# Decoder layer with mixture of experts: the loop for further rounds in front of the last expert group, and joint stores

## The chip, the cores and the metric

The kernel runs on one core of a Trainium2 chip. The metric is device time in microseconds of one execution; the runs before took 459.01 to 460.41 us, median 459.82. Engines are TensorE (PE; its weight loads are PEld), VectorE (DVE), ScalarE (ACT), GpSimd (POOL) and SyncE (SP), which issues most DMAs from one in-order queue.

## The reference

One decoder layer for 256 tokens of width 1024, in float32:

```
h  = RMSNorm(x);  [u|v|q|k|vb] = h @ W_in
y_a = u * (tril(W_s) RMSNorm(v) + b)          # chunks of 128
y_b = differential attention of q, k, vb       # 8 heads, ALiBi, softmax1 - lam*softmax2
x  = x + (sigmoid(h Wg_a)*(y_a Wup_a) + sigmoid(h Wg_b)*(y_b Wup_b)) @ W_out
t  = RMSNorm(x);  group = top-1 of 4, experts = top-2 of the 8 in it
y  = sum over experts e of c[e] * (silu(t w1[e]) * (t w3[e])) @ w2[e]     # 32 experts, hidden 256
out = x + y
```

## The kernel before

**The front.** Projections, mixers, gates and the output projection run as units of weight pieces, each split into a high and a low part. They end near 258 us and are not touched by the change.

**The experts.** The 32 experts are worked in eight groups of four (`run_groups`, `group`). A group takes for each expert at most 32 tokens (`SL`). Its steps, in `group`: `sel` makes a 0/1 matrix `Sg` of tokens by slots on VectorE; `gather` multiplies it with the token rows, which gives the gathered tokens `hT` (two halves of four pieces); `products` multiplies `hT` with w1 and w3, in eight steps `kc` of one weight chunk each, into `h` (L1123); then `hid` (silu on ScalarE, product on VectorE), two transposes `pt`, the copy `hidT`, and the second stage: four chunks of w2 give `y` (L1170), copied to `yy` (L1176), and `comb` scatters it back onto the PSUM banks `res` with the matrix `SwT` (L1149). `back_a` (GpSimd) makes `Sw`, the weighted `Sg`, and `back_b` transposes it to `SwT`. Parts of the next group's preparation are hung into the steps of a group by the table `mids`: entry `kc` runs behind product `kc`, entry `KC + i` behind chunk `i` of the second stage.

**The weight stream.** A group has 12 chunks of 1 MB, 96 in all; I number them 0 to 95, so the last group has 84 to 95. `Stream.pump` issues a transfer on SyncE whenever a slot is free. From chunk 54 on, two chunks go together as one 2 MB transfer into one of six double buffers `sd_70` to `sd_75` (L162), a "double"; chunk 94 is a transfer of its own (L174) and chunk 95 two halves (L156). Chunks 86/87 go to `sd_75`, 88/89 to `sd_70`, 90/91 to `sd_71`, 92/93 to `sd_73`.

**The last group.** It also stores the result: behind each range of 256 or 128 columns, `put_out` copies `res` to a tile `out` (VectorE, in the last ranges also ScalarE) and stores it: six stores in all. Behind each of its product steps 0 to 6 stand 14 matmuls on constants (`warm`, L275), 18 behind step 7; nothing reads their result.

**Further rounds.** An expert with more than 32 tokens needs another round. The kernel counts on the chip how many are needed (`ci`, made in the first group); behind everything each engine loads that count and, if it is over zero, loops over all eight groups again and stores the result once more. With these inputs the loop is not entered. The order of the instructions in front of the loop is written out by hand (`manual_schedule`): each engine works in the order of the code.

Of the kernel before, what the change touches and what calls it, by code (L numbers as in the profile page):

```python
# [7 lines left out]
F32 = mybir.dt.float32  # L8
# [9 lines left out]
P = 128  # L18
D = 1024
T = 256  # L20
NT = 2
KC = 8
# [19 lines left out]
RESERVE = (6, 3, 2, 0, 0, 0, 0, 0, 1)  # L42
SL = 32
NW = (14, 18)

COLS = (((0, 256),), ((512, 256),), ((256, 128), (768, 128)), ((384, 128), (896, 128)))
NGRP = 8
NCH = 12
ROUNDS = T // SL
# [81 lines left out]
def piece(chunk, e):  # L131

    return chunk[e] if isinstance(chunk, tuple) else chunk[:, e * 512:(e + 1) * 512]
# [66 lines left out]
def body(tc, cp, sp, tp, mmp, axp, xT_d, xn_d, wf_d, wm_d, wst_d, bs_d, pv_d, rb_d, wr_d, out_d):  # L200
    nc = tc.nc
    V, S, G, TE = nc.vector, nc.scalar, nc.gpsimd, nc.tensor
    slots = Slots(sp, "s", NSLOT - 3 - 2 * NTWO, NTWO)
# [5 lines left out]
    def ax_ps(name):  # L209
        return axp.tile([P, 512], F32, tag="ax", name=name)  # L210
# [24 lines left out]
    def t1k(shape, name, dt=F32):  # L235
        return tp.tile(shape, dt, tag="t1k", name=name, bufs=6)
# [4 lines left out]
    order = tc.manual_schedule()  # L241
# [3 lines left out]
    stream = Stream(nc, slots, [wf_d[i] for i in range(40)], wm_d, 40 + TWO)  # L245
# [4 lines left out]
    first = [stream.claim() for _ in range(NFIRST)]  # L250
    for a, b in FIRST:
        c = slice(a % 4 * 512, (b - 1) % 4 * 512 + 512)
# [19 lines left out]
    def warm(n):  # L272
        wps = ax_ps("wps")
        for _ in range(n):
            TE.matmul(wps[:, :P], ones_b, ones_b, start=True, stop=True)  # L275
# [8 lines left out]
    for sl_, base in ((slice(0, P), 0), (slice(P, 3 * P), -P)):  # L284
        n = sl_.stop - sl_.start
# [86 lines left out]
    A = {}  # L372
# [495 lines left out]
    res = [[None] * 2 for _ in range(NT)]  # L868
# [171 lines left out]
            evac0(part)  # L1040


    def put_out(c, n):

        o = slots.take([P, NT, n], F32, "out")
        for t in range(NT):
            src = res[t][c // 512][:, c % 512:c % 512 + n]
            if t == 0 and (c, n) in COLS[-1]:
                S.copy(o[:, t], src)
            else:  # L1050
                V.tensor_copy(o[:, t], src)
        nc.sync.dma_start(out_d[0, :, c:c + n].rearrange("(t p) n -> p t n", t=NT), o)
        slots.drop(o)

    def group(g, chunks, done, mid, store):

        es = slice(g * 4, g * 4 + 4)
        st = {"h": [None, None]}

        def sel(ts=range(NT)):  # L1060
            if 0 in ts:
                st["S"] = t1k([P, NT, 4, SL], f"Sg{g}")
            for t in ts:
                V.tensor_tensor(st["S"][:, t], io32p[:, None, :].to_broadcast([P, 4, SL]),  # L1064
                                pos_m[:, t, es, None].to_broadcast([P, 4, SL]), ALU.is_equal)
# [9 lines left out]
                      start=start, stop=t == NT - 1, skip_group_check=True)  # L1075

        def gather_T(hf):
            st["h"][hf] = A["lp"].tile([P, 4, P], F32, tag=f"h{hf}", name=f"hT{g}{hf}")

        def gather_out(hf, ps, ks):  # L1080
            n = len(ks)
# [36 lines left out]
        def products():  # L1118
            ps = ax_ps(f"h{g}")
            for kc in range(KC):  # L1120
                w = chunks()
                for e in range(4):
                    TE.matmul(ps[e * SL:(e + 1) * SL], st["h"][kc // 4][:, kc % 4, e * SL:(e + 1) * SL], piece(w, e),  # L1123
                              start=kc == 0, stop=kc == KC - 1)
                done()
                if store and kc < KC - 1:
                    warm(NW[0])
                for f in mid.get(kc, ()):
                    f()
            if store:  # L1130
                warm(NW[1])
            hid = t1k([P, T], f"hid{g}")
            S.activation(hid, ps[:, :256], AF.Silu)  # L1133
            V.tensor_tensor(hid, hid, ps[:, 256:], ALU.mult)  # L1134
            for f in mid.get("act", ()):
                f()
            pt = ax_ps(f"pt{g}")
            for f in range(2):
                TE.transpose(pt[:, f * P:(f + 1) * P], hid[:, f * P:(f + 1) * P], ident)
            hidT = t1k([P, 2, P], f"hidT{g}")  # L1140
            V.tensor_copy(hidT, pt[:, :256].rearrange("p (f s) -> p f s", f=2))
            for f in mid.get("T", ()):
                f()

            def comb(ranges, yy):
                o = 0
                for c, n in ranges:
                    for t in range(NT):
                        TE.matmul(res[t][c // 512][:, c % 512:c % 512 + n], st["SwT"][:, t * P:(t + 1) * P], yy[:, o:o + n],  # L1149
                                  start=False, stop=True, skip_group_check=True)  # L1150
                    o += n
                    if store:
                        put_out(c, n)

            last = None
            for i, ranges in enumerate(COLS):
                chunk = chunks()
                final = g == NGRP - 1 and i == 3
                o = 0
                for part in [(r,) for r in ranges] if final else [ranges]:  # L1160
                    n = sum(r[1] for r in part)
                    py = ax_ps(f"y{g}{i}{o}")
                    if final:
                        v = chunk[:, o * 8:(o + n) * 8].rearrange("p (e f n) -> p e f n", e=4, f=2)
                        w = [v[:, e] for e in range(4)]
                    else:
                        w = [piece(chunk, e).rearrange("p (f n) -> p f n", f=2) for e in range(4)]
                    for f in range(2):
                        for e in range(4):
                            TE.matmul(py[e * SL:(e + 1) * SL, :n], hidT[:, f, e * SL:(e + 1) * SL], w[e][:, f],  # L1170
                                      start=f == 0, stop=f == 1)
                    o += n
                    if o == 256:
                        done()
                    yy = t1k([P, n], f"yy{g}{i}{o}")
                    S.copy(yy, py[:, :n])  # L1176
                    if last:
                        comb(*last)
                    last = (part, yy)
                    if store and i == 1:  # L1180
                        comb(*last)
                        last = None
                for f in mid.get(KC + i, ()):
                    f()
            if last:
                comb(*last)

        return sel, gather, back_a, back_b, products, gather0, evac0, sel_r2

    def run_groups(next_, done_, first, final):  # L1190
        mids = [{} for _ in range(NGRP)]
        gr = [group(g, next_, done_, mids[g], final and g == NGRP - 1) for g in range(NGRP)]
        sel, gather, back_a, back_b, _, gather0, evac0, sel_r2 = gr[0]
        if first:
            choice_end(sel, gather0, evac0, sel_r2)
        else:
            sel()
            gather(0)
        mids[0][2] = [lambda: gather(1, "Sr" if first else "S")]
        mids[0][3] = [first, back_a] if first else [back_a]  # L1200
        if first:
            mids[0][4] = [lambda t=t: res_init(t, 1) for t in range(NT)]
        mids[0][6] = [back_b]
        for g in range(NGRP):
            if g + 1 < NGRP:
                sel_, gather_, back_a_, back_b_ = gr[g + 1][:4]
                mids[g].setdefault(4, []).append(sel_)

                mids[g]["act"] = [lambda ga=gather_: ga(0)]
                mids[g]["T"] = [lambda ga=gather_: ga(1)]  # L1210
                mids[g][KC + 2] = [back_a_]
                mids[g + 1][1] = [back_b_]
            gr[g][4]()

    def consume(st):

        box = {}

        def next_():
            box["w"] = st.next()  # L1220
            return box["w"]

        def done_():
            slots.drop(box["w"])
            st.pump(0)
        return next_, done_

    ci = cp.tile([P, 1], I32, name="ci")

    def rest():  # L1230
# [11 lines left out]
        V.tensor_reduce(cs, cr, AX.X, ALU.add)  # L1242
        V.tensor_copy(ci, cs)

    run_groups(*consume(stream), rest, True)
    order.__exit__(None, None, None)


    more = nc.values_load(ci[0:1, 0:1], min_val=0, max_val=ROUNDS - 1)
    with tc.If(more > 0):  # L1250
        with tc.For_i(0, more, 1):
            V.tensor_scalar(pos_m, pos_m, -float(SL), None, ALU.add)
            st = Stream(nc, slots, [], wm_d, 0)
            st.pump(0)
            run_groups(*consume(st), None, False)
        for ranges in COLS:
            for c, n in ranges:
                put_out(c, n)
    for name in ("gathered", "extra2", "gates", "extra"):
        close_pool(name)  # L1260

# [62 lines left out]
```

## Time and profile before

| | |
|---|---|
| runs | 459.01 to 460.41 us, median 459.82 |
| profiled execution | 459.95 us, its span 458.2 us |
| busy: TensorE, VectorE, ScalarE, GpSimd | 433.5, 219.6, 184.2, 94.7 us |
| DMA | 148.75 MB, mean 325 GB/s over the span |
| last double landed | 443.53 us |
| end of the last copy | 452.2 us |

Times within the profile count from the start of the span. A view of a stretch lists for each engine the busy time and the number of instructions, then the granted share of TensorE's clock (1.00 is 2.4 GHz, 0.50 is 1.2 GHz). In a list of operations, "[0.41 <-DMA ...]" is the idle time in front and what ended it.

### The profile page before, as it was taken

To read this page: it belongs to the slowest core of one execution; us is meant where nothing else is said; L and a number is where in the kernel's file an instruction comes from. 1 tells how busy PE (TensorE), PEld (TensorE's weight loads), DVE (VectorE), ACT (ScalarE), POOL (GpSimd) and SP (SyncE) were. 2 spreads that over 40 slices of the span, in tenths; PEclk is the share of its full clock that TensorE was granted. 3 is DMA by queue.
4 is the path that set the end of the run, shared out by engine and by line. 5 is a ranking of instruction groups with operands and counts; after the bars stand their busy time and mean duration, and the time that the engine had idled before them with its cause. 6 is when DMAs were issued, how large, how long until landed. Compare 5 with 4: busy or idle time off the path is not lost.

```text
span 458.2 us, 7864 instructions
## 1 busy us (share of the span) xinstructions
PE 433.5 (95%) x3136; PEld 317.8 (69%) x3136; DVE 219.6 (48%) x423; ACT 184.2 (40%) x364; POOL 94.7 (21%) x120
## 2 busy tenths in 40 slices
PE   8999999999999999999999999999999968759984
PEld 6787778878999888888888845475554625307553
DVE  4865696779897766666885633021110201001012
ACT  5946557676565776644565233010100101001001
POOL 1057576446567000004000111000000000000000
PEclk9999999999999999999999999999999999968998
DMA  7999943554327877698776999999999999999993
GB/s 265 415 421 423 406 151 137 183 185 149 129 93 276 349 294 275 240 377 297 297 257 209 393 358 426 418 418 421 406 425 424 428 426 426 426 429 428 423 378 106
DMA packets 23129, 148.75 MB, mean 325 GB/s; under 512 B 2736, under 2 KB 5040, under 8 KB 9136
## 3 DMA queue, kind: packets, MB, share of 16 engines
q1 hardware_dynamic: 22656, 147.91, 81.1%
q8 instruction: 26, 0.43, 0.4%
q10 hardware_dynamic: 432, 0.28, 0.2%
q14 instruction: 15, 0.12, 0.1%
HBM read 147.14 MB, written 1.05 MB: 323 GB/s over the span
## 4 chain that ended last, share of the span: by engine, by line
PE 74%; DMA 20%; DVE 2%; POOL 1%; ACT 1%; issue 1%; SPq 0%
DMA sd<-in_wm_dram 16%; PE h L1123 9%; PE gp L1074 5%; PE y L1170 4%; PE res L1149 4%; PE b L467 3%; PE gb L467 3%; PE ga L467 3%; PE a L467 3%; DMA sd<-in_xn_dram 2%; PE v L419 2%; PE u L448 2%; PE u L449 2%; PE u L450 2%; PE ga L468 2%; PE b L468 2%
## 5 line engine op out<-in xcount | busy, mean ns | idle before, releaser
L404 DVE TENSOR_TENSOR hl<-sd,hl 128x1024 fp32r<-128x1024 f32 (+2 forms) x84 | 87.4, 1046 | 43.0 <-ACT hl L400 40.8
L400 ACT CAST hl<-sd 128x1024 fp32r<-128x1024 f32 (+1 forms) x84 | 80.4, 965 | 63.2 <-PE a L468 8.5
L1123 PE MATMUL h<-sd,hT 128*32 128x512 f32 x384 | 49.9, 630 | 13.8 <-DMA sd<-in_wm_dram 13.8
L1134 DVE TENSOR_TENSOR hid<-hid,h 128x256 f32<-128x256 f32 x8 | 3.4, 422 | 99.2 <-ACT hid L1133 99.2
L406 POOL TENSOR_TENSOR hl<-sd,hl 128x352 fp32r<-128x352 f32 x32 | 40.4, 1274 | 20.8 <-ACT hl L400 20.6
L1176 ACT COPY yy<-y 128x256 f32<-128x256 f32 (+1 forms) x33 | 12.1, 366 | 68.4 <-PE y L1170 68.3
L1123 PEld LDWEIGHTS h<-sd,hT 128*32 128x32 f32 x384 | 10.7, 112 | 38.5 <-issue 19.1
L1109 POOL TENSOR_TENSOR Sw<-Sg,C 128x128 f32<-128x128 f32 x16 | 6.1, 399 | 149.6 <-PE res L1149 140.0
L1149 PE MATMUL res<-yy,SwT 128*128 128x128 f32 (+1 forms) x192 | 34.6, 323 | 0.1
L1074 PEld LDWEIGHTS gp<-Sg,acc 128*128 128x128 f32 x240 | 29.1, 198 | 7.5 <-issue 7.5
L1149 PEld LDWEIGHTS res<-yy,SwT 128*128 128x128 f32 x192 | 25.9, 190 | 10.5 <-issue 6.0
L1074 PE MATMUL gp<-Sg,acc 128*128 128x128 f32 x240 | 31.2, 285 | 0.0
L1133 ACT ACTIVATE hid<-h 128x256 f32<-128x256 f32 x8 | 3.1, 383 | 56.4 <-PE h L1123 56.4
L467 PE MATMUL ga<-x,hl 128*128 128x512 f32 x64 | 22.8, 400 | 0.0
L467 PE MATMUL b<-yb,hl 128*128 128x512 f32 x64 | 22.7, 399 | 0.0
L467 PE MATMUL gb<-x,hl 128*128 128x512 f32 x64 | 22.7, 399 | 0.0
L467 PE MATMUL a<-ya,hl 128*128 128x512 f32 x64 | 22.7, 399 | 0.0
L1170 PE MATMUL y<-sd,hidT 128*32 128x256 f32 x304 | 19.3, 383 | 1.7 <-DMA sd<-in_wm_dram 1.7
L1082 DVE TENSOR_TENSOR hT<-gp,pv 128x512 f32<-128x512 f32 (+1 forms) x19 | 11.3, 606 | 19.9 <-PE gp L1074 19.9
L1064 DVE TENSOR_TENSOR Sg<-io32p,pos_m 128x128 f32<-128x128 f32 x16 | 4.0, 288 | 33.1 <-PE y L1170 33.1
L448 PE MATMUL u<-x,hl 128*128 128x256 f32 x64 | 18.8, 293 | 0.0
L450 PE MATMUL u<-x,hl 128*128 128x256 f32 x64 | 18.1, 283 | 0.0
(226 smaller groups left out, 901.0 us busy)
## 6 DMA issues: line engine op xcount, KB each, us to landing
sd<-in_wm_dram SPq DMA_DIRECT2D x20, 2048.0 KB, 24.1
sd<-in_wf_dram SPq DMA_DIRECT2D x34, 1024.0 KB, 6.4
sd<-in_wm_dram SPq DMA_DIRECT2D x27, 1024.0 KB, 7.9
w<-in_wm_dram SPq DMA_DIRECT2D x24, 1024.0 KB, 10.2
w<-in_wm_dram SPq DMA_DIRECT2D x16, 256.0 KB, 8.9
sd<-in_wf_dram SPq DMA_DIRECT2D x6, 512.0 KB, 7.6
sd<-in_xn_dram SPq DMA_DIRECT2D x2, 1024.0 KB, 9.1
w<-in_wf_dram SPq DMA_DIRECT2D x2, 1024.0 KB, 8.1
```

Of the source, the lines that this page charges most:

```text
L400: S.copy(hl[:, 0, c], raw[:, c])
L404: V.tensor_tensor(hl[:, 1, c.start:m], raw[:, c.start:m], hl[:, 0, c.start:m].bitcast(F32), ALU.subtract)
L406: G.tensor_tensor(hl[:, 1, m:c.stop], raw[:, m:c.stop], hl[:, 0, m:c.stop].bitcast(F32), ALU.subtract)
L448: TE.matmul(o, wh, a[:, 0], start=kc == 0, stop=False)
L450: TE.matmul(o, wl, a[:, 0], start=False, stop=kc == KC - 1)
L467: TE.matmul(ps, wh, a.rearrange("p c t -> p (c t)"), start=kc == 0, stop=False, skip_group_check=True)
L468: TE.matmul(ps[:, :T], wl, a[:, 0], start=False, stop=kc == KC - 1, skip_group_check=True)
L1074: TE.matmul(ps[:, i * P:(i + 1) * P], h2[:, t, kc * P:(kc + 1) * P], st[S_][:, t].rearrange("p e s -> p (e s)"), start=start, stop=t == NT ...
L1123: TE.matmul(ps[e * SL:(e + 1) * SL], st["h"][kc // 4][:, kc % 4, e * SL:(e + 1) * SL], piece(w, e), start=kc == 0, stop=kc == KC - 1)
L1149: TE.matmul(res[t][c // 512][:, c % 512:c % 512 + n], st["SwT"][:, t * P:(t + 1) * P], yy[:, o:o + n], start=False, stop=True, skip_group_ ...
L1170: TE.matmul(py[e * SL:(e + 1) * SL, :n], hidT[:, f, e * SL:(e + 1) * SL], w[e][:, f], start=f == 0, stop=f == 1)
L1176: S.copy(yy, py[:, :n])
```

## The change

Four edits. The last group is cut off from `run_groups` and emitted behind the loop (`last_group`); the count is loaded in group 4 (`count`), and the branch stands between groups 6 and 7. What the last group holds over the loop (its `Sg` and `hT`, and the tiles for the output) gets slots of its own, and the loop's weights use those that are left. Four of the six output ranges are copied into one tile and stored in two transfers, one for each half of the tokens. The matmuls on constants behind steps 0 to 5 of the last group go, and its `back_a` and `back_b` move to its steps 1 and 4.

```diff
+NW_FROM = 6
...
     def put_out(c, n):
-        o = slots.take([P, NT, n], F32, "out")
+        h, k = divmod(c, 512)
+        late = (c, n) in COLS[-1]
         for t in range(NT):
-            src = res[t][c // 512][:, c % 512:c % 512 + n]
-            if t == 0 and (c, n) in COLS[-1]:
-                S.copy(o[:, t], src)
+            src = res[t][h][:, k:k + n]
+            if late and t == 0:
+                S.copy(out_t[c][:, t], src)
+            elif late:
+                V.tensor_copy(out_t[c][:, t], src)
             else:
-                V.tensor_copy(o[:, t], src)
-        nc.sync.dma_start(out_d[0, :, c:c + n].rearrange("(t p) n -> p t n", t=NT), o)
-        slots.drop(o)
+                V.tensor_copy(out_t[0][:, t, h, k:k + n], src)
+        if late:
+            nc.sync.dma_start(out_d[0, :, c:c + n].rearrange("(t p) n -> p t n", t=NT), out_t[c])
+        elif (c, n) == COLS[-2][-1]:
+            o = out_d[0].rearrange("(t p) (h n) -> p t h n", t=NT, h=2)
+            for t in range(NT):
+                nc.sync.dma_start(o[:, t, :, :k + n], out_t[0][:, t])
...
-                st["S"] = t1k([P, NT, 4, SL], f"Sg{g}")
+                st["S"] = slots.take([P, NT, 4, SL], F32, f"Sg{g}") if store else t1k([P, NT, 4, SL], f"Sg{g}")
...
-                if store and kc < KC - 1:
+                if store and NW_FROM <= kc < KC - 1:
                     warm(NW[0])
...
+        if count:
+            mids[4][6] = [count]
...
-                mids[g][KC + 2] = [back_a_]
-                mids[g + 1][1] = [back_b_]
+                if first and g + 2 == NGRP:
+                    mids[g + 1][1] = [back_a_]
+                    mids[g + 1][4] = [back_b_]
+                else:
+                    mids[g][KC + 2] = [back_a_]
+                    mids[g + 1][1] = [back_b_]
+            elif first:
+                return gr[g][4]
             gr[g][4]()
...
-    run_groups(*consume(stream), rest, True)
+    def count():
+        more.append(nc.values_load(ci[0:1, 0:1], min_val=0, max_val=ROUNDS - 1))
+
+    last_group = run_groups(*consume(stream), rest, count)
+    take_out()
     order.__exit__(None, None, None)
-    more = nc.values_load(ci[0:1, 0:1], min_val=0, max_val=ROUNDS - 1)
-    with tc.If(more > 0):
-        with tc.For_i(0, more, 1):
+    with tc.If(more[0] > 0):
+        with tc.For_i(0, more[0], 1):
             V.tensor_scalar(pos_m, pos_m, -float(SL), None, ALU.add)
-            st = Stream(nc, slots, [], wm_d, 0)
+            st = Stream(nc, slots, [], wm_d, NGRP * NCH)
             st.pump(0)
-            run_groups(*consume(st), None, False)
-        for ranges in COLS:
-            for c, n in ranges:
-                put_out(c, n)
+            run_groups(*consume(st), None)
+    order = tc.manual_schedule()
+    order.__enter__()
+    last_group()
+    order.__exit__(None, None, None)
```

SyncE's queue from the double with chunks 86/87 (`sd_75`) on, before; what stands in brackets are the semaphores that an instruction waits for (`DMAHW` those of transfers, the others those of engines):

```order
L162 DMA sd_75<-in_wm_dram 128x4096 [waits DMAHW0_49,PE_49]
L162 DMA sd_70<-in_wm_dram 128x4096 [waits DMAHW1_49,PE_49]
L162 DMA sd_71<-in_wm_dram 128x4096 [waits DMAHW2_49,PE_49]
L162 DMA sd_73<-in_wm_dram 128x4096 [waits DMAHW3_49,PE_49]
L174 DMA w_3742<-in_wm_dram 128x2048
L156 DMA w_3744<-in_wm_dram 128x1024
L156 DMA w_3744<-in_wm_dram 128x1024 [waits DMAHW4_49]
L1052 DMA out_dram<-out_3980 128x2x256 [waits DMAHW5_49,DVE_49]
...
L1249 TENSOR_LOAD ci [waits DVE_49]
L1249 ISA x2
...
L1052 DMA out_dram<-out_4043 128x2x128 [waits DMAHW2_49,DVE_49,Activation_49]
L1250 COMPARE_AND_BRANCH
```

The same place now; the loop's path (the rows left out) is skipped when the count is zero, and the branch with the eight `DMAHW` waits is the path that skips it:

```order
L163 DMA sd_75<-in_wm_dram 128x4096 [waits DMAHW0_49,PE_49]
L1284 COMPARE_AND_BRANCH
...
L1284 UNCONDITIONAL_BRANCH [waits DMAHW0_49,DMAHW1_49,DMAHW2_49,DMAHW3_49,DMAHW4_49,DMAHW5_49,DMAHW6_49,DMAHW7_49]
L163 DMA sd_70<-in_wm_dram 128x4096 [waits DMAHW7_49,DMAHW1_49,PE_49]
L163 DMA sd_71<-in_wm_dram 128x4096 [waits DMAHW2_49,DMAHW0_49,PE_49]
L163 DMA sd_73<-in_wm_dram 128x4096 [waits DMAHW3_49,DMAHW1_49,PE_49]
L175 DMA w_3756<-in_wm_dram 128x2048 [waits DMAHW2_49]
L157 DMA w_3758<-in_wm_dram 128x1024 [waits DMAHW3_49]
L157 DMA w_3758<-in_wm_dram 128x1024 [waits DMAHW4_49]
L1063 DMA out_dram<-out_3797 256x1x384 [waits DMAHW5_49,DVE_49]
...
L1059 DMA out_dram<-out_3798 128x2x128 [waits DMAHW7_49,DVE_49,Activation_49]
```

The transfers of chunks 88 to 95 and the stores stood in front of the branch; they now stand behind it, and behind a wait for every transfer issued so far.

TensorE at the start of the last group, before: products `h` of the first chunk, then the matmuls on constants `wps`:

```order
L1149 MATMUL res_2818<-yy_3776,SwT_3659 128x128
L1149 MATMUL res_2821<-yy_3776,SwT_3659 128x128
L1123 MATMUL h_3786<-sd_74,hT_3703 32x512 [waits DMAHW5_49,PE_49]
L1123 MATMUL h_3786<-sd_74,hT_3703 32x512 x3
L275 LDWEIGHTS ones_b
L275 MATMUL wps<-ones_b 128x128 [waits PE_49]
L275 LDWEIGHTS ones_b
```

TensorE now, from the end of the path that skips the loop to the first matmuls on constants:

```order
L1284 UNCONDITIONAL_BRANCH [waits PE_49]
L1141 MATMUL h_5201<-sd_74,hT_111_3717 32x512 [waits DVE_49,DMAHW5_49,PE_49,Activation_49]
L1141 MATMUL h_5201<-sd_74,hT_111_3717 32x512 x7
L1141 MATMUL h_5201<-sd_75,hT_111_3717 32x512 [waits DMAHW6_49]
L1141 MATMUL h_5201<-sd_75,hT_111_3717 32x512 x7
L1141 MATMUL h_5201<-sd_70,hT_112_3733 32x512 [waits DMAHW7_49]
L1141 MATMUL h_5201<-sd_70,hT_112_3733 32x512 x3
L1132 MATMUL pw_5225<-ident,Sw_5210 128x128 [waits Pool_49] x2
L1141 MATMUL h_5201<-sd_70,hT_112_3733 32x512 x4
L1141 MATMUL h_5201<-sd_71,hT_112_3733 32x512 [waits DMAHW0_49]
L1141 MATMUL h_5201<-sd_71,hT_112_3733 32x512 x3
L276 LDWEIGHTS ones_b [waits PE_49]
L276 MATMUL wps<-ones_b 128x128 [waits Activation_49]
```

The first product now follows the branch, six sets of `wps` are gone, and `pw` (`back_b`) moved from behind the second chunk to behind the fifth.

## Rows read from the trace of the kernel before

**Rows 1.** the page, part 2: tenths of busy time or clock in forty equal slices

```profile
PEclk9999999999999999999999999999999999968998
DMA  7999943554327877698776999999999999999993
```

**Rows 2.** the chain that ended last, 405 to 460: start us, us, what

```profile
408.89 3.64 PE h L1123 x16
...
419.57 23.96 DMA sd<-in_wm_dram
...
443.67 1.93 PE y L1170 x32
...
451.95 0.28 DVE out L1051
```

**Rows 3.** SyncE's timeline, each followed by its issues: KB each, us to landing

```profile
401.08 0.33 SPq L162 DMA_DIRECT2D sd<-in_wm_dram  x1
...
sd<-in_wm_dram SPq DMA_DIRECT2D x1, 2048.0 KB, 27.6
...
420.43 0.91 SPq L156 DMA_DIRECT2D w<-in_wm_dram  x2
...
w<-in_wm_dram SPq DMA_DIRECT2D x2, 512.0 KB, 27.2
```

**Rows 4.** TensorE's timeline, 394 to 452: start us, us, operation, idle before

```profile
399.09 1.92 PE L1123 MATMUL h<-sd,hT 128*32 128x512 f32 x16 [2.35 <-DMA sd<-in_wm_dram]
...
425.55 1.06 PE L1123 MATMUL h<-sd,hT 128*32 128x512 f32 x8
426.55 0.95 PE L275 MATMUL wps<-ones_b 128*128 128x128 bf16 x14
...
433.78 1.06 PE L1123 MATMUL h<-sd,hT 128*32 128x512 f32 x8 [0.41 <-DMA sd<-in_wm_dram]
...
438.67 1.06 PE L1123 MATMUL h<-sd,hT 128*32 128x512 f32 x8 [1.05 <-DMA sd<-in_wm_dram]
...
441.56 1.18 PE L275 MATMUL wps<-ones_b 128*128 128x128 bf16 x18
```

**Rows 5.** stretches: us, busy (x instructions) by engine, PEclk, DMA share, GB/s

```profile
360.00:380.00 20.00, 15.84 (x157) 6.94 (x155) 1.19 (x3) 1.86 (x5) 0.76 (x2) 1.00 1.01 427
...
393.50:404.60 11.10, 4.82 (x42) 1.40 (x46) 0.00 (x0) 0.37 (x1) 0.00 (x0) 1.00 1.01 428
404.60:414.90 10.30, 8.48 (x43) 3.25 (x32) 0.42 (x1) 0.38 (x1) 0.00 (x0) 0.50 1.01 426
414.90:425.50 10.60, 10.60 (x113) 7.55 (x111) 1.71 (x3) 1.49 (x4) 0.76 (x2) 1.00 1.01 427
425.50:435.30 9.80, 9.39 (x110) 4.61 (x109) 0.00 (x0) 0.37 (x1) 0.00 (x0) 1.00 1.00 425
```

**Rows 6.** the branch's lines L1249 and L1250: ns min/median/max, first and last start

```profile
L1249 SPq TENSOR_LOAD <-ci x1: 481/481/481, 451.0 to 451.0; - x1
...
L1250 SPq EVENT_SEMAPHORE  x8: 17/17/17, 453.4 to 456.8; - x8
...
L1250 PEldq COMPARE_BRANCH  x1: 4253/4253/4253, 452.1 to 452.1; - x1
...
L1250 SPq COMPARE_BRANCH  x1: 50/50/50, 452.9 to 452.9; - x1
```

**Rows 7.** DMA, 451 to 457, then the stores issued at 450.1 and 452.4

```profile
DMA  8986985000005995887210010000000000000005
...
q8 instruction: 2, 0.03, 3.3%
q14 instruction: 3, 0.02, 1.2%
...
out_dram<-out SPq DMA_DIRECT2D x1, 128.0 KB, 1.9
...
out_dram<-out SPq DMA_DIRECT2D x1, 128.0 KB, 4.0
```

More of the change, by code (lines that the diff above doesn't have):

```diff
@@ L1040, in choice_end, with take_out @@
             evac0(part)
+    out_t = {}
     def put_out(c, n):
-        o = slots.take([P, NT, n], F32, "out")
+        h, k = divmod(c, 512)
+        late = (c, n) in COLS[-1]
         for t in range(NT):
-            src = res[t][c // 512][:, c % 512:c % 512 + n]
-            if t == 0 and (c, n) in COLS[-1]:
-                S.copy(o[:, t], src)
-            else:
-                V.tensor_copy(o[:, t], src)
-        nc.sync.dma_start(out_d[0, :, c:c + n].rearrange("(t p) n -> p t n", t=NT), o)
-        slots.drop(o)
+            src = res[t][h][:, k:k + n]
[3 more added lines that the diff above has]
+                V.tensor_copy(out_t[c][:, t], src)
+            else:
+                V.tensor_copy(out_t[0][:, t, h, k:k + n], src)
[5 more added lines that the diff above has]
+                nc.sync.dma_start(o[:, t, :, :k + n], out_t[0][:, t])
+    def take_out():
+        c, n = COLS[-2][-1]
+        out_t[0] = slots.take([P, NT, 2, c % 512 + n], F32, "out")
+        for c, n in COLS[-1]:
+            out_t[c] = slots.take([P, NT, n], F32, "out")
     def group(g, chunks, done, mid, store):
@@ L1077, in gather_T @@
         def gather_T(hf):
-            st["h"][hf] = A["lp"].tile([P, 4, P], F32, tag=f"h{hf}", name=f"hT{g}{hf}")
+            st["h"][hf] = (slots.take([P, 4, P], F32, f"hT{g}{hf}") if store else
+                           A["lp"].tile([P, 4, P], F32, tag=f"h{hf}", name=f"hT{g}{hf}"))
         def gather_out(hf, ps, ks):
@@ L1188, in group, with run_groups @@
         return sel, gather, back_a, back_b, products, gather0, evac0, sel_r2
-    def run_groups(next_, done_, first, final):
+    def run_groups(next_, done_, first, count=None):
         mids = [{} for _ in range(NGRP)]
-        gr = [group(g, next_, done_, mids[g], final and g == NGRP - 1) for g in range(NGRP)]
+        gr = [group(g, next_, done_, mids[g], first and g == NGRP - 1) for g in range(NGRP)]
         sel, gather, back_a, back_b, _, gather0, evac0, sel_r2 = gr[0]
@@ L1243, in rest @@
         V.tensor_copy(ci, cs)
-    run_groups(*consume(stream), rest, True)
+    more = []
+    def count():
+        more.append(nc.values_load(ci[0:1, 0:1], min_val=0, max_val=ROUNDS - 1))
+    last_group = run_groups(*consume(stream), rest, count)
+    take_out()
     order.__exit__(None, None, None)
-    more = nc.values_load(ci[0:1, 0:1], min_val=0, max_val=ROUNDS - 1)
-    with tc.If(more > 0):
-        with tc.For_i(0, more, 1):
+    with tc.If(more[0] > 0):
+        with tc.For_i(0, more[0], 1):
             V.tensor_scalar(pos_m, pos_m, -float(SL), None, ALU.add)
-            st = Stream(nc, slots, [], wm_d, 0)
+            st = Stream(nc, slots, [], wm_d, NGRP * NCH)
             st.pump(0)
-            run_groups(*consume(st), None, False)
-        for ranges in COLS:
-            for c, n in ranges:
-                put_out(c, n)
+            run_groups(*consume(st), None)
[3 more added lines that the diff above has]
+    order.__exit__(None, None, None)
     for name in ("gathered", "extra2", "gates", "extra"):
```

## The prediction

> **What bounds the kernel now.** I read the page's forty slices first: from slice 23 on the DMA row stands at nine tenths until the last slice, and PEclk is full except for a dip in slices 36 and 37 and the very end [rows 1]. Then the chain that ended last: its two long pieces near the end are weight transfers, the last one until 443.53, and what follows is the tail of products, stores and barrier [rows 2]. So the last 200 us run at the rate of the weight stream, and the end is that stream's last double chunk (92 and 93) plus what TensorE, ScalarE, VectorE and the stores still do behind it: 443.67 to 458.2, 14.5 us.
>
> Third, the issues. The double with chunks 86 and 87 is issued at 401.08 and lands 27.6 us later, at 428.7; the last piece of chunk 95 is issued at about 420.9 and lands some 27.2 us later, at 448.1 to 448.5 [rows 3]. The queue thus holds five transfers ahead of use and never runs empty: 8 MB in some 19.8 us. TensorE's products of the last group wait for that stream at 433.78 (chunk 88) and 438.67 (chunk 90) [rows 4], and the second stage starts at 443.67, right behind the landing [rows 2]. A double comes every 4.9 us.
>
> Fourth, the end. The last VectorE copy ends at 452.2 [rows 2]. Stores of 128 KB land 1.9 us after issue before that, but 4.0 us when issued at 452.4 [rows 7], next to the branch: TensorE's COMPARE_BRANCH takes 4253 ns [rows 6], five instruction fetches on two queues lie in that stretch, and from 454 to 456 only a trickle is left on the DMA engines [rows 7]. I read this as one DMA engine that is held by the fetches and finishes its share late.
>
> **The change part by part.**
>
> *The loop in front of the last group.* In the order, SyncE now meets the branch after the double 86/87, and on the path that skips the loop it waits for all eight DMA semaphores before it issues 88/89, 90/91, 92/93, 94 and 95. Before, those were issued from 407 on, behind others. So the queue runs dry at 428.7. What a restart costs: a 128 KB store lands 1.9 us after its issue [rows 7]; its bytes take 0.3 us at the 425 GB/s of the stretch [rows 5], so 1.6 us are latency, and SyncE's wake-up about 0.1. I take +1.7 us for every later landing: 88/89 at 435.4, 90/91 at 440.3, 92/93 at 445.2, and the last piece near 450.2. Bounds: 0.4 us (only an issue of 0.33 [rows 3] and the wake-up, all latency hidden) and 6 us (SyncE's skip is short there, 50 ns, but TensorE's takes 4253 ns [rows 6]: if SyncE's code has to be fetched after the wait, it comes on top). I stand near the store row, because SyncE reaches the branch soon after 401 and can take its jump while it waits.
>
> TensorE, VectorE, ScalarE and GpSimd jump too. For TensorE I take the 4.25 us of its row, from 425.6 to about 429.9. Behind it stand the products of chunks 84 to 87, four times about 1.0 us [rows 4], done by 434.3, before 88 lands at 435.4. Cost nothing; without that cover (a fetch 2 us slower beside the weight stream) chunks 88 and 89 are late, but 90 waits for its data until 440.3 anyway. GpSimd's Sw and the transposes pw move from the end of group 6 and chunk 1 to chunks 1 and 4: they lie in the same wait and are needed only at the second stage.
>
> *The warm-up matmuls.* The fillers after chunks 0 to 5 of the last group go: six times 14, each set about 0.9 us [rows 4]. They stood in waits, so their time is worth nothing. What they did is hold the clock. In group 6, which has no fillers, TensorE was busy 4.82 of 11.1 us and the granted clock then fell to 0.5 (1.2 GHz) from 404.6 to 414.9; in the last group, with fillers, it was busy 9.39 of 9.8 us and the clock stayed at 1.0 [rows 5]. After the change the same stretch, 425.5 to 435.3, holds four products (4.0 us) and little else: as thin as group 6. So I expect the clock to fall near 435 and, as in the row, to stay low some 10 us, to about 446. The price, from rows at either level: a double's sixteen products take 1.92 us at full clock and 3.64 at half [rows 2, 4], so a chunk 1.8 instead of 1.0. From chunk 90 at 440.3: product 1.8, 14 fillers 1.7 (their 0.9 doubled), product 1.8, which ends at 445.6. From there, over the 18 fillers, hid, its transposes and the copy hidT, it is 2.1 us to the second stage now (441.56 to 443.67 [rows 2, 4]); I take 2.3, since the clock returns within it. The second stage starts at about 447.9 instead of 443.67: +4.2, of which 1.7 is the restart and 2.5 the clock. The landing of 92/93 at 445.2 is covered by this. Bounds of the clock term: 0 (it holds) and 4 (the tail begins at half clock as well).
>
> *The end.* No branch, no loop path behind the stores. The last stores should land 1.9 us after issue, not 4.0: −2.1. SyncE's eight semaphore waits on the skipping path, 453.4 to 456.8 with the last six after the landing, go: −0.4 [rows 6]. TENSOR_LOAD of the counter (481 ns on SyncE, between two stores [rows 6]) hid in a wait. Against this, four stores become two of 384 KB each, issued about 1.5 us ahead of the last two: 0.79 MB need 1.85 us at the stream's rate, so the last ones queue about 0.2 behind them. I take −2.3 in sum; bounds −2.9 and −0.5 (the stores stay slow, because TensorE's next code comes then). Separate out slots also end the wait of the last copy for a store's landing, but TensorE's last product ended only then: nothing.
>
> *The counter's load in group 4.* Each engine loads a register there (SyncE's load takes 481 ns at the end [rows 6]). The weight stream runs on, and the later stretch 360 to 380 has TensorE busy 15.84 of 20 us [rows 5], so the loss is taken back: 0, at most 0.8.
>
> The profiled execution took 459.95 us (span 458.2), 0.13 over the median of the runs. Sum: 459.95 + 1.7 + 2.5 − 2.3 = **461.9 us**.
>
> **A rule that bears on the jump.** On the trace, TensorE's taken branch cost 4.25 us and SyncE's 0.05 [rows 6]; which of them a jump gets is what I can't read off for the new place. The Trainium skill, Runtime: NRT & Kernel Launch, section Instruction fetch mechanics, says that a taken branch to a target outside the code already fetched has to wait for that page by DMA. The trace agrees for TensorE (4253 ns); and SyncE's loop body is now over three times as long, so by that rule its jump would stall too. That is the third rival.
>
> **The rivals.**
> 1. *The clock holds* (not slower). For it: the fillers after chunks 6 and 7 remain and the end of group 6 was dense (10.60 of 10.60 us busy before 425.5 [rows 5]). Against it: the group 6 row. Then only the restart and the end count: 459.95 + 1.7 − 2.3 = 459.35, no change.
> 2. *The queue restarts almost for nothing and the clock holds.* Place: SyncE's wait at 428.7. If the latency is hidden to the 0.4 bound and the end gives 2.3, the time is 458.05, faster. It decides once the restart is under 0.8 us. Against it: 1.9 us for a store with an empty queue.
> 3. *SyncE's jump stalls after its wait.* 88/89 then lands at 439.7, 90/91 at 444.6, 92/93 at 449.5; the second stage starts at about 449.9, +6.2, and the sum is 459.95 + 6.2 − 2.3 = 463.85. For it: TensorE's row; against it: SyncE reaches the branch over 20 us early, and the waits and the next issues stand directly behind each other.
>
> **How the numbers follow.** Forecast 0.55 (own range 460.6 to 463.2), rival 1 0.25, rival 2 0.08, rival 3 0.12. A measurement of this kernel tells a change from none at about 0.3%, 1.4 us: faster is under 458.4, slower over 461.2. Of the forecast's 0.55 about 0.44 lies over 461.2 and 0.11 below; rival 1 puts 0.19 in the middle and 0.06 under 458.4. So faster 0.14, same 0.30, slower 0.56. The range 458.6 to 463.8 leaves out rival 2, the low edge of rival 1 and half of rival 3.
>
> **What would show it.** In the trace after: a hole of 1 to 3 us in the DMA rate near 429 and the issues of the last doubles behind it instead of at 407 to 420; TensorE idle about 4 us between groups 6 and 7; a granted clock of 0.5 from about 435 to 446; the second stage of the last group starting near 448; the last store landing within 2.5 us. I am wrong if the clock stays at 1.0 through the last group, if the stream shows no hole, or if the last stores still take 4 us.

## The result and the profile after

The changed kernel takes 462.62 us (median of 5 runs, 462.21 to 464.88) against 459.92 before: a ratio of 1.0062, 95% interval 1.0044 to 1.0079. It is 0.6% slower, near the 461.9 of the forecast. Its profiled execution took 462.21 us, 2.26 over the one of before, with a span of 460.5. The total came out, its terms did not: one was too small, one was not there, one was too large.

Page, part 2, of the kernel after, to be set against [rows 1]:

```profile
PEclk9999999999999999999999999999999998979799
DMA  7999943554327977798776999999999999999694
```

The DMA row has a hole (six tenths) in slice 38, where nine tenths stood before. The clock's dip of before, slices 36 and 37, has become three small ones, in 34, 36 and 38; the last of them lies beside the hole.

The chain of after, late part (start us, us, what), against [rows 2]:

```profile
429.80 0.33 SPq L163
...
430.27 12.31 DMA sd<-in_wm_dram
...
447.62 1.93 PE y L1188 x32
...
455.94 0.29 DVE out L1055
```

Before, the piece of weight transfer ran back to 419.57. Now it begins at 430.27, with SyncE's issue in front of it: the stream starts anew there. The second stage starts at 447.62 instead of 443.67, +3.95. From there to the end of the span it takes 12.9 us instead of 14.5, −1.65. The two make the +2.3 of the profiled executions.

SyncE's timeline, and from the DMA view the issue of 88/89 (KB, us to landing), both against [rows 3]; then the branch's line (ns min/median/max, first and last start), against [rows 6]:

```profile
429.80 2.53 SPq L163 DMA_DIRECT2D sd<-in_wm_dram  x3
```

```profile
sd<-in_wm_dram SPq DMA_DIRECT2D x1, 2048.0 KB, 7.9
```

```profile
L1284 SPq EVENT_SEMAPHORE  x8: 17/17/17, 409.4 to 429.7; - x8
...
L1284 SPq COMPARE_BRANCH  x1: 45/45/45, 404.0 to 404.0; - x1
...
L1284 PEldq COMPARE_BRANCH  x1: 5277/5277/5277, 424.1 to 424.1; - x1
```

SyncE jumps at 404.0 in 45 ns, waits for eight semaphores until 429.7, when 86/87 is in, and only then issues 88/89. From this issue to the landing it takes 7.9 us. From landing to landing, 86/87 (429.58) to 88/89 (437.73), it is 8.15 us; before, this gap was 5.1 and the next ones 4.9. So the restart costs 3.1 against the trace of before, and 3.25 against the usual step. TensorE's jump takes 5.28 us. The DMA view of 425 to 440, forty slices of 0.375 us, shows the hole itself:

```profile
DMA  5946621201000209915599898998989989989999
```

The engines run short of work from slice 6 (426.9) on, 2.7 us before the last byte of 86/87 is reported and SyncE may go on, and are full again from slice 21 (432.5), 2.7 us behind the issue. In the trace of before, the next double's bytes stand on both sides: 425 GB/s over the same stretch [rows 5].

TensorE's timeline (start us, us, operation, idle before), against [rows 4], and stretches (columns as in [rows 5]):

```profile
429.79 6.12 PE L1141 MATMUL h<-sd,hT 128*32 128x512 f32 x32 [4.23 <-PEq L1284]
437.77 1.07 PE L1141 MATMUL h<-sd,hT 128*32 128x512 f32 x8 [1.85 <-DMA sd<-in_wm_dram]
...
442.63 1.06 PE L1141 MATMUL h<-sd,hT 128*32 128x512 f32 x8 [2.43 <-DMA sd<-in_wm_dram]
...
445.51 1.18 PE L276 MATMUL wps<-ones_b 128*128 128x128 bf16 x18
```

```profile
425.50:435.30 9.80, 5.57 (x29) 1.48 (x32) 0.00 (x0) 0.00 (x0) 0.76 (x2) 0.65 0.59 218
435.30:443.60 8.30, 4.02 (x34) 0.67 (x26) 0.00 (x0) 0.37 (x1) 0.00 (x0) 1.00 1.01 430
...
428.10:434.80 6.70, 5.01 (x24) 1.35 (x28) 0.00 (x0) 0.00 (x0) 0.76 (x2) 0.50 0.62 218
```

The stream's rate falls from 425 to 218 GB/s over 425.5 to 435.3. The clock is at its lower level (0.50, 1.2 GHz) from 428.1 to 434.8, inside the jump and the products of 84 to 87; those 32 take 6.12 us and are done 1.85 us before chunk 88 is in. From 434.9 on the clock is full again, and chunk 90 takes 1.06 us, not the 1.8 of the forecast.

The last store of after (KB, us to landing) and its line, against [rows 7]:

```profile
out_dram<-out SPq DMA_DIRECT2D x1, 128.0 KB, 2.8
```

```profile
L1059 SPq DMA_DIRECT2D out_dram<-out x2: 491/698/905, 455.8 to 456.4; - x2
```

It lands 2.8 us after issue, not 4.0 and not 1.9, and the issue itself takes 905 ns.

### The profile page after: what moved, and what is told of

Same layout as the page of the kernel before. It is cut to its first block, busy times and chain, and to the rows that moved or that the text cites. A ratio compares the mean times of both kernels' runs of the same rounds, so it can differ in the third digit from the quotient of the medians.

```text
span 460.5 us, 7694 instructions
## 1 busy us (share of the span) xinstructions
PE 431.3 (94%) x3052; PEld 314.2 (68%) x3052; DVE 219.5 (48%) x423; ACT 184.2 (40%) x364; POOL 94.2 (20%) x120
## 5 line engine op out<-in xcount | busy, mean ns | idle before, releaser
L1141 PE MATMUL h<-sd,hT 128*32 128x512 f32 x384 | 51.7, 657 | 21.0 <-DMA sd<-in_wm_dram 13.8
L1134 ACT COPY SwT<-pw 128x256 f32<-128x256 f32 x8 | 3.0, 372 | 40.5 <-PE pw L1132 40.5
```

## The experiments

Ratios are to the kernel before, run on the same chip beside them, with 95% intervals.

**1. The stream not cut.** The hand-written order is not closed ahead of the branch, so SyncE issues 88 to 95 before it meets the branch:

```
     take_out()
-    order.__exit__(None, None, None)
     with tc.If(more[0] > 0):
...
-    order = tc.manual_schedule()
-    order.__enter__()
     last_group()
```

> The changed kernel with one edit: the hand-written order is not closed in front of the branch, so SyncE issues the transfers of chunks 88 to 95 before it meets the branch; the branch itself stays between groups 6 and 7. Theory 1 (the drained weight queue is the whole loss): no hole in the DMA rate near 429, 88/89 lands 5.0 us behind 86/87 instead of 8.15, the second stage of the last group starts near 444.3, and the time falls by about 3 us from the changed kernel, to 459 or just under (ratio to before 0.994 to 1.000). Theory 2 (the jump of TensorE or its clock is the loss): TensorE still jumps for about 5 us and still has no fillers before chunk 90, so the time stays within 1 us of the changed kernel's 462.6.

Measured: 463.51, ratio 1.0077 (1.0048 to 1.0105). There is no hole in the stream (88/89 lands 4.96 us behind 86/87), as theory 1 has it, and no gain, as theory 2 has it. TensorE's timeline of this kernel:

```profile
429.81 0.99 PE L1141 MATMUL h<-sd,hT 128*32 128x512 f32 x1 [4.97 <-PEq L1281]
435.33 6.84 PE L1141 MATMUL h<-sd,hT 128*32 128x512 f32 x39 [4.53 <-issue]
```

Behind its jump TensorE does one product and then stands 4.53 us more, waiting for nothing that the profile shows. The data were there (88/89 landed at 433.8); TensorE had become the bound: its second stage starts at 448.28, 4.7 us behind the landing of 92/93. A code fetch of 1.10 us begins at 432.96, within this wait. Experiment 5 takes this up.

**2. All fillers back** in the changed kernel (`NW_FROM = 0` instead of 6).

> The changed kernel with the matmuls on constants behind chunks 84 to 89 back. Theory 1 (the drain): they lie in TensorE's wait for 88/89 and 90/91, the landings do not move, the time is that of the changed kernel, 462.6 within 1 us. Theory 2 (the clock that fell without them costs time): the clock stays up from 435 on and the time falls by 1.5 to 2.5 us.

Measured: 463.63, ratio 1.0078 (1.0049 to 1.0106). The clock was low at the same place, 428.4 to 435.3, with the fillers, and they push chunk 90 back: it starts at 444.07, though its data landed at 442.12, and the second stage starts 0.8 us behind the landing of 92/93.

```profile
433.65 1.84 PE L1141 MATMUL h<-sd,hT 128*32 128x512 f32 x8
...
444.07 1.06 PE L1141 MATMUL h<-sd,hT 128*32 128x512 f32 x8
...
449.01 1.93 PE L1188 MATMUL y<-sd,hidT 128*32 128x256 f32 x32 [0.52 <-DVE hidT L1159]
```

Since the changed kernel's second stage starts 0.14 us behind the landing without these fillers, they had nothing to give back: the clock term of the forecast is refuted for this kernel. The profiled execution, at 465.33 the longest of its five, shows something else: from the second stage to the end of the span (463.6) it takes 14.6 us, as before the change, though no branch stands there. Its last two stores land 4.8 and 4.5 us after issue, and a code fetch of 0.95 us begins among them, at 459.81. Whether that fetch delays them was not tried.

**3. No branch at all** in the changed kernel; leaves out the counter load, the branch and the loop for further rounds.

```
-    last_group = run_groups(*consume(stream), rest, count)
+    last_group = run_groups(*consume(stream), rest)
...
-    with tc.If(more[0] > 0):
-        with tc.For_i(0, more[0], 1):
```

> The changed kernel without branch, loop and counter load (it leaves out the further rounds, which these inputs do not need). Theory 1: no hole, and the end keeps its gain of about 1.7 us (stores land 2 to 2.8 us after issue, no skipping path): 458.0 to 458.5, ratio to before about 0.9965; the same as the kernel with the transfers issued ahead of the branch, within 0.5 us. Theory 2 (TensorE's jump costs time): 1 us or more under that kernel.

Measured: 460.65, ratio 1.0006 (0.9991 to 1.0022), 2.2 above the expected range, and 2.9 under experiment 1, as theory 2 has it. Its TensorE timeline shows the clock term after all, where the stream is not cut:

```profile
439.33 1.38 PE L1141 MATMUL h<-sd,hT 128*32 128x512 f32 x8 [2.46 <-DMA sd<-in_wm_dram]
440.64 1.68 PE L276 MATMUL wps<-ones_b 128*128 128x128 bf16 x14
442.25 1.59 PE L1141 MATMUL h<-sd,hT 128*32 128x512 f32 x8
...
445.84 1.93 PE L1188 MATMUL y<-sd,hidT 128*32 128x256 f32 x32 [0.59 <-DVE hidT L1159]
```

Fillers 1.68 instead of 0.95, products 1.38 and 1.59 instead of 1.06. The second stage starts 1.6 us behind the landing of 92/93, not 0.14. This accounts for a part of the 2.2 (experiment 7); the stream is late too, as the last part of the next section says.

**4. The kernel before with the fillers thinned** as in the change.

```
-                if store and kc < KC - 1:
+                if store and 6 <= kc < KC - 1:
```

> The kernel before with the one edit that the matmuls on constants behind chunks 84 to 89 are left out. The prediction's clock term (2.5 us) says: the clock falls near 435 and stays low over chunks 90 and 91, second stage 2 to 2.5 us later, 462.0 to 462.5. Rival (the low stretch falls into waits, as in the changed kernel): 459.9 within 0.7 us, second stage near 443.7.

Measured: 461.2, ratio 1.0026 (1.0007 to 1.0044): 1.2 us, half of the forecast's 2.5. The granted clock was 0.50 from 439.1 to 442.5, 3.4 us and not 10, over chunk 91 and the fillers ahead of it:

```profile
439.14 1.67 PE L275 MATMUL wps<-ones_b 128*128 128x128 bf16 x14
440.75 1.93 PE L1123 MATMUL h<-sd,hT 128*32 128x512 f32 x8
```

**5. The uncut stream with the branch's exit moved.** Experiment 1 with 24 products in the loop's body, which does not run:

```
             V.tensor_scalar(pos_m, pos_m, -float(SL), None, ALU.add)
+            warm(24)
```

> As the kernel with the weight stream not cut at the branch (88 to 95 issued ahead of it), with 24 more matrix products written into the body of the loop for further rounds, which does not run with these inputs; they move the place in TensorE's code where the branch comes out by 48 instructions and change nothing else. Theory 1 (the drained queue is the loss of the change; the second stall of 4.53 us in the uncut kernel was a second code fetch, because TensorE came out two instructions ahead of the end of a fetched piece): TensorE stands 4.2 to 5.3 us at the branch and then works without a stall, the products of 84 to 87 begin near 429.8 and end by 436, the second stage starts at 443.6 to 445.5, and the time is 457.8 to 460.0, ratio 0.995 to 1.000. Rival A (the second stall came because a code fetch stands behind the weight stream in a busy queue, wherever the branch comes out): again some 4.5 us of stall behind one or a few products and 463 to 464, ratio 1.007. Rival B (the drain is not what the change costs): no second stall, and still 461.5 to 463.

Measured: 458.95, ratio 0.9979 (0.9966 to 0.9992). Theory 1 holds in the time and in the one stall, and rivals A and B fall; only the second stage of the profiled execution, at 445.90, lies past the expected 445.5. TensorE's timeline:

```profile
430.00 5.87 PE L1141 MATMUL h<-sd,hT 128*32 128x512 f32 x40 [4.97 <-PEq L1281]
...
439.39 1.74 PE L1141 MATMUL h<-sd,hT 128*32 128x512 f32 x8 [2.16 <-SPq L1281]
441.06 1.67 PE L276 MATMUL wps<-ones_b 128*128 128x128 bf16 x14
```

The same jump, and then forty products in a row: the second stall hung on where the branch came out. A code fetch begins at nearly the same time as in experiment 1 (432.99, 1.07 us), but here TensorE has products to do until it is in. The Trainium skill, Runtime: NRT & Kernel Launch, section Instruction fetch mechanics, has code fetched in blocks of 16 KiB or 256 instructions, whose crossing is mostly hidden. An edge of such a block right behind the exit of experiment 1 fits both traces, though no trace shows where the edges lie; and if it was such a crossing, it was not hidden, it cost 4.53 us. Against the changed kernel (1.0062) the uncut stream with its exit moved is worth 0.83%, 3.8 us. In this profiled execution, at 460.54 one of the longest of its twelve, the clock term (1.74, 1.67) is there too.

**6. Experiment 5 with fillers from chunk 88 on** (`NW_FROM = 4`).

> As the kernel with the uncut stream and the moved exit of the branch, with the 14 fillers behind chunks 88 and 89 as well as 90 and 91. Theory 1 with a clock that matters behind the jump: the fillers keep the products of 90 and 91 at full speed, the second stage starts within 0.5 us of the landing of 92/93 and the time is 457.5 to 458.8, 0.5 to 1.4 us under the same kernel without them. Rival (TensorE, 5 us late out of its jump, has no room for 1.9 to 3.4 us of fillers): the second stage starts 1 to 2.5 us later than without them and the time is 459.5 to 461.5. If the second stall is there whatever the place of the exit, 463.5 to 466.

Measured: 459.4, ratio 0.9987 (0.9975 to 0.9999). Inconclusive: in its trace the clock holds and the second stage starts 0.13 us behind the landing, but the median lies 0.6 above the expected range and not under experiment 5's.

**7. No branch, all fillers** (experiment 3 with `NW_FROM = 0`).

> As the kernel without branch, loop and counter load (it leaves out the further rounds, which do not run with these inputs), with the fillers behind chunks 0 to 5 of the last group put back. Theory (the end of the change is worth 1.7 to 2.1 us by itself; without fillers the clock took 1.4 us of that back): the second stage starts at 443.6 to 444.4 and the time is 457.5 to 458.7, ratio 0.994 to 0.997. Rival (the fillers cost nothing and hold nothing; the 1.4 us belong to the stream): as without them, 460.3 to 460.9, ratio 1.000.

Measured: 459.2, ratio 0.9981 (0.9970 to 0.9993), 0.5 above the expected range. The fillers are worth 0.25%, 1.2 us, here, and the second stage is right behind the landing again (444.73). From it to the end 12.5 us.

**8. The dry queue alone.** Experiment 3, with SyncE waiting for 86/87 before it issues 88/89; the load of a value nobody uses leaves only its wait:

```
+                if self.i == n - 8:
+                    self.nc.values_load(self.sent[0:1, 0:1].bitcast(I32), engines=(mybir.EngineType.SP,))
                 self.nc.sync.dma_start(x[0], self.pairs[self.i])
+                self.sent = x[0]
```

> As the kernel without branch, loop and counter load, with one wait more: SyncE waits for the landing of chunks 86 and 87 before it issues 88/89, so the queue runs dry there as at the branch, and TensorE has no jump. Theory 1 (the drained queue costs 2.5 to 3.1 us by itself): 88/89 lands 7.6 to 8.3 us behind 86/87, not 4.9, the second stage starts 1.5 to 3 us later than without the wait, and the time is 462.0 to 463.8, ratio 1.004 to 1.008. Rival C (the 3 us were TensorE's and the other engines' code fetches in the same queues, and a dry queue alone costs the 1.7 us of a small store's latency or less): 88/89 lands 6.0 to 6.7 us behind 86/87 and the time is 460.7 to 461.8.

Measured: 463.51, ratio 1.0077 (1.0053 to 1.0101), where experiment 3 had 1.0006. Its TensorE timeline:

```profile
430.35 2.88 PE L1144 MATMUL h<-sd,hT 128*32 128x512 f32 x16 [2.20 <-DMA sd<-in_wm_dram]
437.94 1.93 PE L1144 MATMUL h<-sd,hT 128*32 128x512 f32 x8 [4.71 <-DMA sd<-in_wm_dram]
```

Chunk 88 comes 7.59 us behind chunk 86, not 4.9: 2.7 us for a dry queue, with no jump on TensorE near it. Rival C (1.7 or less) falls. Where the other 0.5 of the changed kernel's 3.25 comes from was not tried.

**9 and 10. Six stores instead of four**, in experiment 5 (9) and in experiment 7 (10):

```
-        if late:
-            nc.sync.dma_start(out_d[0, :, c:c + n].rearrange("(t p) n -> p t n", t=NT), out_t[c])
-        elif (c, n) == COLS[-2][-1]:
...
+        nc.sync.dma_start(out_d[0, :, c:c + n].rearrange("(t p) n -> p t n", t=NT),
+                          out_t[c] if late else out_t[0][:, :, h, k:k + n])
```

> As the kernel with the uncut stream and the moved exit of the branch (458.95, ratio 0.9979), but with the first four output ranges stored one by one as before the change (six stores instead of four). In that kernel SyncE is busy from the first joint store on without a break and the last store's issue takes 915 ns and lands 2.8 us after its start; before, the last issues took 375 and 409 ns. Theory S (joining the stores is what makes the last issue slow, since 0.79 MB are issued in a row just ahead of it): the last issue takes 0.4 to 0.5 us, lands 1.9 us after its start, and the time is 458.0 to 458.6. Rival (the last issue is slow whatever stands ahead of it, so joining costs nothing): 458.7 to 459.3, ratio as without this edit. Rival 2 (joining gives something, as fewer stores queue ahead of the last): 459.4 to 460.

> As the kernel without branch, loop and counter load and with all fillers (459.2, ratio 0.9981; it leaves out the further rounds, which do not run with these inputs), but with six stores as before the change. Theory S: the last store lands 0.5 to 0.9 us earlier against the second stage's start, and the time is 458.3 to 458.8, ratio 0.996 to 0.9975. Rival (joining costs nothing): 459.0 to 459.5, ratio 0.998. Rival 2 (joining gives something): 459.6 to 460.1.

Measured: 457.43, ratio 0.9955 (0.9943 to 0.9968), and 458.45, ratio 0.9971 (0.9959 to 0.9983). Theory S holds; experiment 9 even lies 0.6 under its range, and its profiled execution, unlike that of experiment 5, has no clock term (chunk 90 takes 1.06 us). The stores' line of experiment 9 (ns min/median/max), its last store in the DMA view, and its second stage in TensorE's timeline:

```profile
L1058 SPq DMA_DIRECT2D out_dram<-out x6: 372/389/447, 449.0 to 452.5; - x6
```

```profile
out_dram<-out SPq DMA_DIRECT2D x1, 128.0 KB, 1.9
```

```profile
443.81 1.93 PE L1184 MATMUL y<-sd,hidT 128*32 128x256 f32 x32 [0.58 <-SPq L1277]
```

No issue takes over 447 ns, and the last store lands after 1.9 us. From the second stage to the end (span 455.6) it is 11.8 us, and 12.9 with the joint stores (experiment 5): joining costs 1.1 us. Between experiments 10 and 7 it is 11.6 against 12.5, 0.9. Experiment 9 beats both kernels, by 0.45% and 1.1%.

**11. The kernel before without its branch**, its counter load and its loop for further rounds, which it leaves out.

```
-    more = nc.values_load(ci[0:1, 0:1], min_val=0, max_val=ROUNDS - 1)
-    with tc.If(more > 0):
...
```

> The kernel before without its branch, loop and counter load at the end, and nothing else changed (it leaves out the further rounds, which do not run with these inputs). Theory (the end's gain of the change comes from taking the branch away from the last stores: they then land 1.9 us after issue and not 4.0, and the skipping path's waits of 0.4 go): from the start of the second stage to the end of the span 12.0 to 12.6 us instead of 14.5, and the time is 457.4 to 458.2, ratio 0.9945 to 0.9965. Rival (the stores are slow for another reason, and what the changed kernels gain at the end comes from the separate output tiles or the joint stores): 13.8 to 14.5 us, 459.2 to 460. It also shows once more how far the weight stream runs late in a kernel that is the same up to its end: theory, within 0.5 us of the trace of before at the landing of chunk 86; rival (the changed kernels' streams run late by 0.4 to 1.7 us through an edit of the change), the same as before's and never later.

Measured: 458.5, ratio 0.9975 (0.9965 to 0.9986), 0.3 above the expected range. Its stores' line, and its second stage in TensorE's timeline:

```profile
L1052 SPq DMA_DIRECT2D out_dram<-out x6: 372/383/421, 448.1 to 453.3; - x6
```

```profile
444.67 1.93 PE L1170 MATMUL y<-sd,hidT 128*32 128x256 f32 x32 [0.64 <-DMA sd<-in_wm_dram]
```

From there to the end of the span (456.2) it takes 11.6 us instead of 14.5 (14.6 in experiment 12): in these traces the branch beside the last stores cost 3.0 us. The second stage itself is 1.0 late, in a kernel that is the same up to its end, so the lateness does not come from an edit in the last group. In the medians only 0.25%, 1.2 us, is left of the gain.

**12. The kernel before once more**, unchanged.

> The kernel before, unchanged, profiled once more. In the first trace of it chunk 86/87 lands at 428.66; in all kernels derived from the changed one it lands 0.15 to 1.65 later, and the lateness is there from the first 30 us on, where the programs are alike; the kernel before without its branch shows 1.19. If the stream's start differs from execution to execution, this trace may show anything from 428.3 to 430.3, and its span moves with it (457.8 to 459.8); a landing over 429.0 shows it. If the lateness belongs to the kernels whose end was changed, it lands at 428.3 to 428.8 again, and the question stays open, since one trace more is weak evidence.

One execution, 460.23. Its stores' line with their time to landing, and its second stage in TensorE's timeline:

```profile
L1052 SPq DMA_DIRECT2D out_dram<-out x6: 372/412/1845, 447.4 to 453.4; - x6
...
DMA to landing us min/median/max: 2.2/3.6/3.9
```

```profile
443.90 1.93 PE L1170 MATMUL y<-sd,hidT 128*32 128x256 f32 x32 [0.66 <-DMA sd<-in_wm_dram]
```

86/87 landed at 429.07, 0.4 later than in the first trace, and the second stage started 0.2 later, so part of the lateness differs by execution. The end takes 14.6 us again, though in another form: here an issue takes 1845 ns, there the landing took 4.0 us.

## Why the prediction was right, and where its steps failed

- **The queue's restart (+1.7): the mechanism right, mis-sized.** Landing to landing it measured 3.1 in the changed kernel (3.25 against the usual step) and 2.7 with no branch beside it (experiment 8). The step took the latency of one small store as the price, counted from the landing. But the engines idle on both sides of it, for want of the next double before and in starting up after. It was inside the bounds (0.4 to 6). The cut is the loss: without it, and with the exit moved off the second stall, the change is no slower than before (experiment 5, ratio 0.9979).
- **The clock (+2.5): the step that failed.** "I expect the clock to fall near 435 ... to stay low some 10 us": it fell at 428.1, was back at 434.9, and all of the low time lay in the jump and ahead of chunk 88, which was late anyway. Fillers did not bring a gain there (experiment 2). The effect exists where the stream is not cut (experiments 3, 4 and 5), but it is 1.2 us in the median (experiment 4, and 3 against 7), and the low stretch over chunks 90 and 91 lasts some 3.4 us. The group 6 row from which the 10 us were read was no measure for this place; in the trace after, group 6 itself has two low stretches of 3.4 us (from 400.7 and from 411.0). Rival 1 thus had the clock's price right, at nothing, and its time (459.35) wrong, by the restart and the late stream.
- **The end (−2.3): two terms against each other.** Taking the branch away is worth 3.0 in the traces (experiment 11), not 2.5; the joint stores cost 0.9 to 1.1 (experiments 9 and 5, 10 and 7), not 0.2, since the last store is issued in 905 ns behind them and lands after 2.8, past the 2.5 that was to show the gain. The sum was −1.65; some 0.25 of it is not assigned. Nor is the gain safe: in the trace of experiment 2 it is gone without a branch.
- **TensorE's jump (cost nothing): right, by its cover.** It took 5.28 us, not 4.25, and 6.0 to 6.5 beside a full queue, in the uncut kernels. The products behind it were still done 1.85 us ahead of chunk 88. Without the hole that cover is thin: a second stall of 4.53 us ate the whole gain of experiment 1.
- **SyncE's jump (rival 3) did not stall:** 45 ns, taken 25.7 us ahead of the last wait, as its "against" had it.
- **The sum:** 459.95 + 0.9 (stream late: 86/87 lands at 429.58, not 428.66) + 3.1 (restart) + 0 (clock) − 1.65 (end) = 462.3, measured 462.21. Forecast: 459.95 + 1.7 + 2.5 − 2.3. The errors of +1.4, −2.5, +0.65 and the 0.9 that was not in it cancel to under 0.5: the time was right by compensation.

What stays open is the 0.9 of the late stream. The landing of 86/87 lies between 0.3 ahead of the first trace and 1.65 behind it, and the difference is there from the first 30 us on, where all programs are alike. It has an order that goes with the branch. A weight transfer that lands at 24.1 us in the first trace lands 1.2 to 1.55 us later in the five kernels without a branch (experiments 3, 7, 8, 10 and 11), and between 0.2 ahead and 0.95 behind in all nine traces with one. So the kernels without a branch carry most of a microsecond that arises long before their last group, and their times understate what they save at the end; why their streams start late no run shows. The changed kernel has a branch, and its 0.4 at that transfer and 0.9 at 86/87 lie within the spread of the nine; a single trace of each does not tell a cause from chance there. The median gap of 2.7 us asks for some lateness, or for a clock term in some executions.

## What to carry to other kernels

Before code with a branch is moved into a running stream, look at what the engine that issues the transfers has to wait for on the skipping path: issue the rest of the stream ahead of it, or the queue runs dry, which cost about 3 us here. A branch beside the last stores cost as much in the traces; between two groups it is cheap only while TensorE's jump has cover, and the place where it comes out cost another 4.5 us in one kernel. A saving at the end has to be looked for in more than one trace. Stores at the tail are better small and early than joined, as the last one is issued more slowly and lands later behind them.

## What the runs showed of the hardware

- A TensorE branch took 3.96 and 4.25 us at the quiet end, 5.28 and 6.52 as the queue ran dry (the changed kernel and experiment 2), and 6.02 to 6.48 with the queue full (experiments 1, 5, 6 and 9); on SyncE, ScalarE and GpSimd it took 45 to 50 ns, on VectorE 72. Code fetches use the DMA engines beside the weights: of the 294 packets between 425 and 440 in the changed kernel, two on q8 and one on q14 are such fetches.
- 48 instructions of code that never runs moved a kernel by 4.5 us (ratio 1.0077 to 0.9979) (experiments 1 and 5).
- A weight queue of 2 MB transfers that ran dry and started again lost 2.7 us (experiment 8) and 3.1 to 3.25 us (the changed kernel).
- A store of 128 KB was issued in 372 to 447 ns and landed after 1.9 us with little ahead of it; 905 ns and 2.8 us behind two of 384 KB (experiment 9 and the changed kernel).
